# First FFN's up projection: a quad's first weights in a tile of their own, one weight sum by GpSimd, the last product on the banks of its sum

## The chip, the core and the metric

The kernel runs on one core of one Trainium2 chip. The metric is the device time of one launch in microseconds, as the median of three runs. The engines are named as the profile names them: PE is TensorE (PEld its weight loads), DVE is VectorE, ACT is ScalarE, POOL is GpSimd, and SP is SyncE, which here only issues DMAs. Each engine runs its instructions in the order in which they stand in the program. An instruction whose operand is not there yet holds up all that stand behind it on its engine.

## What is computed

One transformer layer for 256 context tokens and 256 latent tokens of width 2048: a SwiGLU feed-forward half step, a token mixer (attention and an mLSTM), and a second feed-forward half step. The change touches the first feed-forward:

```python
def half_step_ffn(x, mod, i, g, w_up, w_down):
    h = adaln(x, g, mod, i)
    a, b = jnp.split(h @ w_up, 2, axis=-1)
    return x + 0.5 * mod[:, i + 2, None, :] * ((jax.nn.silu(a) * b) @ w_down)
```

It runs on both token streams, so on 512 tokens, with `w_up` of 2048 x 11264 and `w_down` of 5632 x 2048. The vectors `mod` (nine shifts, scales and gates for each stream) are products of a condition vector with a 2048 x 18432 matrix, and they are needed only later, which is why part of their work is put beside the up projection.

## The kernel before

All matrix products are done in float32 precision by splitting each operand into a high part `hi` and a remainder `lo` (`split`, L94): ScalarE writes `hi`, VectorE writes `lo = raw - hi`, both for 128x1024 at a time, and `mm3` (L122) issues three matmuls, hi with hi, hi with lo, lo with hi. The `hi` and `lo` tiles have four buffers each, so two weight tiles of 128x2048 are split at any time.

The hidden dimension is cut into 11 blocks of 512 columns. Block 0 is done early; blocks 1 to 10 are each done by one call of `quad(n)` (L749). A quad multiplies the tokens (two halves of 128 for each stream `s`) by the gate columns (`ab` = 0) and the value columns (`ab` = 1) of its block, with the depth of 2048 in two halves. That would be eight block products; a Winograd scheme does it with seven, at the price of sums of tokens (`n1`, `s2`, `s4`, `s3`, made once) and sums of weights (made in each quad). `order` (L806) lists the seven; each runs in two steps, `q` = 0 and 1, one 1 MB weight tile a step, so that a quad has 14 steps. A step is 24 matmuls of 128x512. Steps are counted 0 to 13 below.

The weights of a quad are eight tiles, `part(n, ab, c)` (L658), c = 0..3 along the depth. Two tiles `chain_[0]` and `chain_[1]` hold the running sums. They start as part (0, q) (`first_chain`, L661), are used by product 0, get (1, q) added by an accumulating DMA that GpSimd's queue issues (`accum`, L642), are used by product 2, get (1, 2+q) added, are used by product 4, get (0, 2+q) added and are used by product 6. After that they are loaded anew for the next quad (`again`, L789). The other four tiles come into the `raw` pool of three buffers: (0, 2+q) for product 1 (`plain`, L800), (1, 2+q) for product 3 (`loaded`, L795), to which (1, q) is then added in place by an accumulating DMA for product 5. Eight accumulating DMAs and six plain ones, of 1 MB each, are thus issued in a quad.

The outputs collect in PSUM banks X, Y and Z, one for each stream. `p1` and `c11` make the gate value of the first token half, `p35` and `c12` (L770) its value part, and their product is queued in `turn`. `kept` and `c22` (L775) make the value part of the second half: `c22` adds X into `cy` on VectorE and copies X into `ca` on ScalarE. Product 6 goes to fresh banks Y, and `c21` (L780) adds Y to `ca`, takes SiLU, and multiplies. `turned` (L731) transposes a finished tile on TensorE and stores it to DRAM.

Beside it runs `side` (L835), made by `mod_items` (L195): 96 items, each a load of 128x1024 of the modulation matrix into `sraw` (two buffers, SP's queue, L212) and two multiply-and-accumulate instructions on VectorE, one for each stream's condition vector in `cBh` (`mod_half`, L180). Their product itself is not wanted; it is written as bf16 to a `c12` tile (`junk`), the same two-buffer pool from which `p35` takes `cb`. One step of `side` is taken at each step of a quad (`after`, L822); the pace is given as (items, steps), and `WAIT` more steps are left after each load of condition vectors (L178). VectorE keeps these instructions in program order. `Beside` (L249) and `mod_late` (L242) use the same `WAIT` and `mod_half` in the mixer and in the second feed-forward.

The down projection (`pair`, L945) has the same seven products for pairs of blocks. There `x3` adds X to two column blocks of the accumulator, and `c21` adds Y, product 6's fresh banks, to one of them.

Of the kernel before, what the change touches and what calls it, by code (L numbers as in the profile page):

```python
# [11 lines left out]
BF16 = mybir.dt.bfloat16  # L12
# [20 lines left out]

WAIT = 2
BLOCKS = ((0, 2), (2, 4), (4, 8), (8, 12), (12, 16))
# [13 lines left out]
def tile_layer(ctx: ExitStack, tc: tile.TileContext, I: dict, out: bass.AP):  # L49
# [130 lines left out]
    def mod_half(raw, cB, junk, i, seqs, kt, h):  # L180

        for s in seqs:
            ins = nc.vector.scalar_tensor_tensor(junk() if junk else raw, raw, 1.0, cB[s], op0=ALU.mult, op1=ALU.mult, accum_out=mT[:, i, s, kt, h : h + 1])  # L183
            tc.keep_in_program_order(ins)
# [434 lines left out]
    def pinned(ins):  # L619
        tc.keep_in_program_order(ins)  # L620
# [22 lines left out]
    with pool(name="f1u", bufs=1) as f1u:  # L643
# [5 lines left out]
        def ca_tile():  # L649
            return f1u.tile([P, CB], F32, tag="ca", name="ca", bufs=2)  # L650
# [7 lines left out]
        def part(n, ab, c):  # L658
            return I["w_up1b"][n - 1, ab, c]

        def first_chain(n, c):  # L661
            nc.sync.dma_start(chain_[c], part(n, 0, c))

# [85 lines left out]
        def quad(n, after=lambda step: None):  # L749

            X, Y, Z = {}, {}, {}
            ca, cy, cb, ra = {}, {}, {}, {}

# [21 lines left out]
            def c22(s):  # L775
                add(cy[s], X[s], cy[s])
                ca[s] = ca_tile()
                nc.scalar.activation(ca[s], X[s], AF.Copy)

            def c21(s):  # L780
                add(ca[s], Y[s], ca[s])
                nc.scalar.activation(ca[s], ca[s], AF.Silu)
                mul(ca[s], ca[s], cy[s])
                turn.append((n, 2 * s + 1, ca[s]))
# [9 lines left out]

            def loaded(q):  # L795
                ra[q] = raw_tile()
                nc.sync.dma_start(ra[q], part(n, 1, 2 + q))
                return ra[q]

            def plain(q):  # L800
                r = raw_tile()
                nc.sync.dma_start(r, part(n, 0, 2 + q))
                return r

            held = lambda q: chain_[q]
            order = (  # L806
                (a11, held, X, True, chained(1, 0), p1),
                (a12, plain, Z, True, None, c11),
                (n1, held, Y, True, chained(1, 2), kept),
                (s4, loaded, Y, False, lambda q: accum(ra[q], part(n, 1, q)), p35),  # L810
                (s2, held, X, False, chained(0, 2), c12),
                (s3, lambda q: ra[q], X, False, None, c22),
                (a22, held, Y, True, again, c21),
            )
            for m, (a, src, dst, fresh, then, use) in enumerate(order):
                if fresh:
                    dst.update({s: bank() for s in range(2)})
                for q in range(2):
                    wt = split(src(q))
                    if then:  # L820
# [13 lines left out]
        cond = Conditions(lambda h: h, lambda h: conditions(halves, h, h + 1), lambda h: halves)  # L834
        side = mod_items(half_items(2, 5), nc.sync.dma_start, sraw, 2, cond, lambda: c12_tile().bitcast(BF16), ((96, (NB - 2) * 14 + 2),))  # L835

# [19 lines left out]

        raws, place0 = [], []
        quad(1, first_steps)
        for n in range(2, NB - 1):
# [85 lines left out]
    def pair(p):  # L945
# [36 lines left out]
        def x3(c, s):  # L982
            put(2 * s + 1, 2 * c, X[c, s], True)
            put(2 * s + 1, 2 * c + 1, X[c, s])
            through_gate(2 * s + 1, 2 * c + 1)

        def c21(c, s):
            put(2 * s + 1, 2 * c, Y[c, s])
            through_gate(2 * s + 1, 2 * c)
# [10 lines left out]
        def b22(c):  # L1000
# [14 lines left out]
            ("s3", lambda c: ra[c], X, False, None, x3),  # L1015
            ("a22", held, Y, True, again, c21),
        )
# [863 lines left out]
```

## Time and profile before

| what | value |
|---|---|
| time, median of 3 runs (lowest to highest) | 2709.36 us (2709.25 to 2710.56) |
| the profiled execution's own time | 2715.45 us |
| its span, first to last instruction | 2713.7 us |
| mean granted TensorE clock | 0.990 |
| ScalarE busy, share of the span | 1270.5 us, 47% |
| VectorE busy, share of the span | 1993.7 us, 73% |
| GpSimd busy, share of the span | 177.0 us, 7% |
| HBM read | 626.31 MB |

The profile is of one execution. Its views give, for each engine, the busy time, groups of equal instructions, and the idle time before an instruction with the event that ended it ("waited for"). A window is a stretch in us from the span's start; its row gives the busy time of each engine, the granted TensorE clock and the mean share of time in which the core's 16 DMA engines were busy. Matmuls are pipelined, so a matmul's own duration is longer than the distance to the next one. A DMA row gives the time from issue to landing, which includes waiting behind other transfers.

### The profile page before, as it was taken

The numbers are of one execution on the slowest core, as the hardware profiler recorded it, in microseconds if no ns is written. First come the engines' busy times: TensorE is split into PE (matmuls) and PEld (weight loads), VectorE is DVE, ScalarE is ACT, GpSimd is POOL, SyncE is SP. The second block draws the span as 40 slices with busy tenths as digits, with TensorE's granted clock in tenths as the row PEclk, the third lists the DMA queues.
The fourth block names the chain that finished last, engine by engine and source line by source line (L and its number), as shares of the span: only waits on it lengthen the run. The fifth ranks groups of instructions, "written<-read, shape, count | busy, mean of one in ns | idle before, by whom it ended". The sixth has DMA issues, their size and how long they took to land. (4 is left out here: it accounts for less than half of the span.)

```text
span 2713.7 us, 33046 instructions
## 1 busy us (share of the span) xinstructions
PE 2635.2 (97%) x12573; PEld 2173.0 (80%) x12573; DVE 1993.7 (73%) x2740; ACT 1270.5 (47%) x1592; POOL 177.0 (7%) x223
## 2 busy tenths in 40 slices
PE   6999999999999999999999999999999999999998
PEld 3588878787888778888889888877898888888886
DVE  2387777777878788888886989787675665666557
ACT  3444444444445455444454346355564444444444
POOL 0000001100101000000110000120000000000000
PEclk8999999999999999999999999999999999999999
DMA  8879999998999989888986867574566666666553
GB/s 354 315 231 251 246 271 263 253 277 240 267 261 273 267 235 247 211 219 224 234 244 230 310 229 239 186 250 154 190 233 219 225 226 222 222 227 217 211 196 128
DMA packets 125311, 644.27 MB, mean 237 GB/s; under 512 B 13400, under 2 KB 17496, under 8 KB 67680
## 3 DMA queue, kind: packets, MB, share of 16 engines
q1 hardware_dynamic: 104704, 508.98, 51.8%
q0 software_dynamic: 20448, 133.18, 24.8%
q8 instruction: 99, 1.62, 0.2%
q14 instruction: 60, 0.49, 0.1%
HBM read 626.31 MB, written 15.79 MB: 237 GB/s over the span
## 5 line engine op out<-in xcount | busy, mean ns | idle before, releaser
L103 DVE TENSOR_TENSOR lo<-raw,hi 128x1024 fp32r<-128x1024 f32 (+3 forms) x600 | 720.0, 1206 | 400.0 <-ACT hi L102 385.5
L102 ACT ACTIVATE hi<-raw 128x1024 fp32r<-128x1024 f32 (+3 forms) x600 | 624.6, 1044 | 762.5 <-PE mm L126 628.1
L125 PE MATMUL mm<-lo,hhi 128*128 128x512 f32 (+3 forms) x1024 | 391.3, 382 | 17.0 <-DVE lo L103 16.9
L124 PE MATMUL mm<-hi,hhi 128*128 128x512 f32 (+3 forms) x1024 | 392.1, 386 | 0.0
L126 PE MATMUL mm<-hi,hlo 128*128 128x512 f32 (+3 forms) x1024 | 389.5, 380 | 0.0
L102 ACT ACTIVATE hi<-chain 128x1024 fp32r<-128x1024 f32 x240 | 252.1, 1058 | 266.7 <-PE mm L126 127.0
L103 DVE TENSOR_TENSOR lo<-chain,hi 128x1024 fp32r<-128x1024 f32 x240 | 289.9, 1222 | 104.0 <-ACT hi L102 101.9
L183 DVE SCALAR_TENSOR_TENSOR c<-sraw,cBh 128x1024 bf16<-128x1024 f32 x192 | 229.6, 1220 | 43.0 <-DMA sraw<-in_w_mt 33.2
L124 PE MATMUL mm<-hi,h2hi 128*128 128x512 f32 x640 | 249.3, 390 | 0.0
L126 PE MATMUL mm<-hi,h2lo 128*128 128x512 f32 x640 | 249.2, 389 | 0.0
L125 PE MATMUL mm<-lo,h2hi 128*128 128x512 f32 x640 | 249.2, 389 | 0.0
L125 PEld LDWEIGHTS mm<-lo,hhi 128*128 128x128 f32 x1024 | 194.1, 190 | 54.0 <-DVE lo L103 23.1
L126 PEld LDWEIGHTS mm<-hi,hlo 128*128 128x128 f32 x1024 | 193.8, 189 | 33.6 <-issue 0.2
L124 PEld LDWEIGHTS mm<-hi,hhi 128*128 128x128 f32 x1024 | 193.1, 189 | 31.4
L124 PE MATMUL mm<-hhi,hi 128*128 128x512 f32 (+1 forms) x384 | 142.0, 371 | 1.2 <-ACT hi L102 1.2
L124 PEld LDWEIGHTS mm<-hi,h2hi 128*128 128x128 f32 x640 | 120.2, 188 | 25.1
L126 PEld LDWEIGHTS mm<-hi,h2lo 128*128 128x128 f32 x640 | 120.2, 188 | 24.9
L125 PEld LDWEIGHTS mm<-lo,h2hi 128*128 128x128 f32 x640 | 120.2, 188 | 24.8
L124 PE MATMUL mm<-hi,hid2h 128*128 128x512 f32 x352 | 138.6, 396 | 0.0
L126 PE MATMUL mm<-hhi,lo 128*128 128x512 f32 (+1 forms) x384 | 137.6, 360 | 1.0 <-DVE lo L103 1.0
L125 PE MATMUL mm<-hlo,hi 128*128 128x512 f32 (+1 forms) x384 | 138.1, 360 | 0.0
L126 PE MATMUL mm<-hi,hid2l 128*128 128x512 f32 x352 | 137.2, 390 | 0.0
(383 smaller groups left out, 4745.7 us busy)
## 6 DMA issues: line engine op xcount, KB each, us to landing
raw<-in_w_up2b SPq DMA_DIRECT2D x80, 1024.0 KB, 4.7
raw<-in_w_dn SPq DMA_DIRECT2D x70, 1024.0 KB, 4.8
sraw<-in_w_mt SPq DMA_DIRECT2D x128, 512.0 KB, 6.4
chain<-in_w_up1b POOLq DMA_DIRECT2D x60, 1024.0 KB, 11.1
raw<-in_w_up1b SPq DMA_DIRECT2D x40, 1024.0 KB, 8.5
sr<-in_w_mt SPq DMA_DIRECT2D x69, 512.0 KB, 5.2
mraw<-in_w_m SPq DMA_DIRECT2D x32, 1024.0 KB, 7.5
chain<-in_w_dn POOLq DMA_DIRECT2D x30, 1024.0 KB, 8.6
```

The costliest lines, as they stand in the source:

```text
L102: nc.scalar.activation(hi, src, AF.Copy)
L103: nc.vector.tensor_tensor(lo, src, hi.bitcast(F32), op=ALU.subtract)
L124: nc.tensor.matmul(out_ap, sh, mh, start=first, stop=False, skip_group_check=skip)
L125: nc.tensor.matmul(out_ap, sh, ml, start=False, stop=False, skip_group_check=skip)
L126: nc.tensor.matmul(out_ap, sl, mh, start=False, stop=last, skip_group_check=skip)
L183: ins = nc.vector.scalar_tensor_tensor(junk() if junk else raw, raw, 1.0, cB[s], op0=ALU.mult, op1=ALU.mult, accum_out=mT[:, i, s, kt, h : ...
```

## The change

In the first feed-forward's up projection:

- The tile of a quad's first product is no longer the chain. `load` puts part (0, 0), (0, 1) and (0, 2) of the next quad into `raw` buffers at steps 8, 11 and 12, and part (0, 3), (1, 2) and (1, 3) of this quad at steps 1, 2 and 4; the table `loads` fixes where they stand. Three loads are issued ahead of the first quad.
- The chain starts as part (1, q). Part (0, q) is added by an accumulating DMA at steps 0 and 1, which no longer has to wait for a split of the chain.
- The sum with part (1, 2+q) is made by GpSimd as an addition in SBUF of 128x2048 (`twice`, steps 6 and 7), from the `raw` tile that product 3 uses, and no longer by an accumulating DMA. The accumulating DMA into that `raw` tile follows it. A quad now has six accumulating DMAs, eight plain ones and two GpSimd additions.
- Product 6 accumulates on the banks X. `c22` no longer copies X, and `c21` applies SiLU to X itself.
- The second of an item's two multiply-and-accumulate instructions writes its product over the `sraw` tile, in float32.
- `WAIT` is 3 in place of 2, and the pace of `side` is 96 items in four steps fewer.

In the down projection, product 6 accumulates on X too, and one of the additions into the accumulator goes.

```diff
@@ -31,7 +31,7 @@
 PACE = 0.5
 
 
-WAIT = 2
+WAIT = 3
 BLOCKS = ((0, 2), (2, 4), (4, 8), (8, 12), (12, 16))
 FB = 4
 CB = 512
@@ -180,7 +180,7 @@
     def mod_half(raw, cB, junk, i, seqs, kt, h):
 
         for s in seqs:
-            ins = nc.vector.scalar_tensor_tensor(junk() if junk else raw, raw, 1.0, cB[s], op0=ALU.mult, op1=ALU.mult, accum_out=mT[:, i, s, kt, h : h + 1])
+            ins = nc.vector.scalar_tensor_tensor(raw if s == seqs[-1] else junk(), raw, 1.0, cB[s], op0=ALU.mult, op1=ALU.mult, accum_out=mT[:, i, s, kt, h : h + 1])
             tc.keep_in_program_order(ins)
 
     def mod_sum(dst, i, s, kk):
@@ -659,7 +659,14 @@
             return I["w_up1b"][n - 1, ab, c]
 
         def first_chain(n, c):
-            nc.sync.dma_start(chain_[c], part(n, 0, c))
+            nc.sync.dma_start(chain_[c], part(n, 1, c))
+
+        raw_of = {}
+
+        def load(n, ab, c):
+            if n < NB:
+                raw_of[n, ab, c] = raw_tile()
+                nc.sync.dma_start(raw_of[n, ab, c], part(n, ab, c))
 
         for c in range(2):
             first_chain(1, c)
@@ -749,7 +756,7 @@
         def quad(n, after=lambda step: None):
 
             X, Y, Z = {}, {}, {}
-            ca, cy, cb, ra = {}, {}, {}, {}
+            ca, cy, cb = {}, {}, {}
 
             def p1(s):
                 ca[s] = ca_tile()
@@ -774,12 +781,10 @@
 
             def c22(s):
                 add(cy[s], X[s], cy[s])
+
+            def c21(s):
                 ca[s] = ca_tile()
-                nc.scalar.activation(ca[s], X[s], AF.Copy)
-
-            def c21(s):
-                add(ca[s], Y[s], ca[s])
-                nc.scalar.activation(ca[s], ca[s], AF.Silu)
+                nc.scalar.activation(ca[s], X[s], AF.Silu)
                 mul(ca[s], ca[s], cy[s])
                 turn.append((n, 2 * s + 1, ca[s]))
 
@@ -792,30 +797,30 @@
                 else:
                     nc.sync.dma_start(chain_[q], I["w_dn1"][0, 2 * q])
 
-            def loaded(q):
-                ra[q] = raw_tile()
-                nc.sync.dma_start(ra[q], part(n, 1, 2 + q))
-                return ra[q]
-
-            def plain(q):
-                r = raw_tile()
-                nc.sync.dma_start(r, part(n, 0, 2 + q))
-                return r
+            def twice(q):
+
+                ra = raw_of[n, 1, 2 + q]
+                pinned(nc.gpsimd.tensor_tensor(chain_[q], chain_[q], ra, op=ALU.add))
+                accum(ra, part(n, 1, q))
 
             held = lambda q: chain_[q]
+            raw = lambda ab, c: lambda q: raw_of[n, ab, c + q]
+            loads = {1: (n, 0, 3), 2: (n, 1, 2), 4: (n, 1, 3), 8: (n + 1, 0, 0), 11: (n + 1, 0, 1), 12: (n + 1, 0, 2)}
             order = (
-                (a11, held, X, True, chained(1, 0), p1),
-                (a12, plain, Z, True, None, c11),
-                (n1, held, Y, True, chained(1, 2), kept),
-                (s4, loaded, Y, False, lambda q: accum(ra[q], part(n, 1, q)), p35),
+                (a11, raw(0, 0), X, True, chained(0, 0), p1),
+                (a12, raw(0, 2), Z, True, None, c11),
+                (n1, held, Y, True, None, kept),
+                (s4, raw(1, 2), Y, False, twice, p35),
                 (s2, held, X, False, chained(0, 2), c12),
-                (s3, lambda q: ra[q], X, False, None, c22),
-                (a22, held, Y, True, again, c21),
+                (s3, raw(1, 2), X, False, None, c22),
+                (a22, held, X, False, again, c21),
             )
             for m, (a, src, dst, fresh, then, use) in enumerate(order):
                 if fresh:
                     dst.update({s: bank() for s in range(2)})
                 for q in range(2):
+                    if 2 * m + q in loads:
+                        load(*loads[2 * m + q])
                     wt = split(src(q))
                     if then:
                         then(q)
@@ -832,7 +837,7 @@
 
         halves = [cBh[:, q, :] for q in range(2)]
         cond = Conditions(lambda h: h, lambda h: conditions(halves, h, h + 1), lambda h: halves)
-        side = mod_items(half_items(2, 5), nc.sync.dma_start, sraw, 2, cond, lambda: c12_tile().bitcast(BF16), ((96, (NB - 2) * 14 + 2),))
+        side = mod_items(half_items(2, 5), nc.sync.dma_start, sraw, 2, cond, lambda: c12_tile().bitcast(BF16), ((96, (NB - 2) * 14 - 2),))
 
         def first_steps(step):
             if step in (1, 2, 3, 4, 5, 6):
@@ -855,6 +860,8 @@
                 split_to(place0[step - 11], quarters(raws[step - 11].bitcast(F32))[0])
 
         raws, place0 = [], []
+        for c in range(3):
+            load(1, 0, c)
         quad(1, first_steps)
         for n in range(2, NB - 1):
             quad(n, lambda step: steps(side))
@@ -980,12 +987,11 @@
             through_gate(2 * s, 2 * c + 1)
 
         def x3(c, s):
-            put(2 * s + 1, 2 * c, X[c, s], True)
             put(2 * s + 1, 2 * c + 1, X[c, s])
             through_gate(2 * s + 1, 2 * c + 1)
 
         def c21(c, s):
-            put(2 * s + 1, 2 * c, Y[c, s])
+            put(2 * s + 1, 2 * c, X[c, s], True)
             through_gate(2 * s + 1, 2 * c)
 
         def loaded(m, cb):
@@ -1013,7 +1019,7 @@
             ("s4", b22, Y, False, lambda c: accum(ra[c], w(0, 2 * c + 1)), p35),
             ("s2", held, X, False, lambda c: accum(chain_[c], w(1, 2 * c)), c12),
             ("s3", lambda c: ra[c], X, False, None, x3),
-            ("a22", held, Y, True, again, c21),
+            ("a22", held, X, False, again, c21),
         )
         todo = first_plan if p == 0 else plan if p < NP - 1 else last_plan
         for m, (g, src, dst, fresh, then, use) in enumerate(order):
```

## The prediction, made before the changed kernel had run

> **What bounds the kernel now.** I first read the page's busy shares, then the first feed-forward in windows: quads, each from its first matmul on `n1` to the next quad's, then all of them in one, then the down projection.
>
> ```profile
> PE 2635.2 (97%) x12573; PEld 2173.0 (80%) x12573; DVE 1993.7 (73%) x2740; ACT 1270.5 (47%) x1592; POOL 177.0 (7%) x223
> ```
>
> ```profile
> core 0: us, PE busy (x) PEld busy (x) DVE busy (x) ACT busy (x) POOL busy (x), PEclk, DMA share, GB/s
> 193.40:271.50 78.10, 78.10 (x353) 64.67 (x352) 57.30 (x69) 37.97 (x44) 7.01 (x8) 1.00 0.94 242
> 349.90:432.00 82.10, 80.05 (x353) 65.83 (x352) 64.31 (x82) 37.88 (x44) 6.95 (x8) 0.98 0.95 266
> 594.20:680.90 86.70, 80.36 (x353) 65.67 (x352) 61.93 (x78) 37.61 (x43) 7.03 (x8) 0.98 0.91 248
> 193.40:987.00 793.60, 770.70 (x3419) 632.66 (x3418) 617.59 (x786) 370.64 (x427) 67.79 (x77) 0.99 0.95 259
> 985.00:1410.00 425.00, 423.76 (x1879) 350.44 (x1877) 362.40 (x411) 212.59 (x237) 51.22 (x60) 1.00 0.90 231
> ```
>
> TensorE sets the end. A quad in which it never waits takes 78.1 us (first window): 14 steps of 5.6 us with the transposes, 5.4 without. The stretch 193.4 to 987.0 holds nine whole quads and the last ten steps of a tenth, 78.1 x (9 + 10/14) = 758.7 us by that measure. It took 793.6. So 34.9 us are lost here, and that is all the change can win in this stage. The DMA engines are busy 0.95 of it. The down projection has nothing to win: PE is busy 423.76 of 425.
>
> The waits in the up projection (160 to 990) say who is late, TensorE's first, then VectorE's: us, times, longest.
>
> ```profile
> PE mm L125 <- DVE lo L103: 22.1, 10, 5.2
> ```
>
> ```profile
> DVE lo L103 <- ACT hi L102: 122.5, 86, 4.0
> DVE c L183 <- DMA sraw<-in_w_mt: 33.2, 15, 7.8
> DVE c L183 <- DMA cBh<-ccd: 9.4, 2, 5.0
> ```
>
> TensorE waits ten times, always for a `lo`. VectorE is not short of time (617.59 of 793.6 us busy); it is held by its order. One such stall in time order, on VectorE and then on TensorE:
>
> ```profile
> 387.24 1.22 DVE L183 SCALAR_TENSOR_TENSOR c<-sraw,cBh 128x1024 bf16<-128x1024 f32 x1
> ...
> 390.52 1.23 DVE L183 SCALAR_TENSOR_TENSOR c<-sraw,cBh 128x1024 bf16<-128x1024 f32 x1 [2.05 <-DMA sraw<-in_w_mt]
> ...
> 392.82 1.22 DVE L103 TENSOR_TENSOR lo<-raw,hi 128x1024 fp32r<-128x1024 f32 x1
> ```
>
> ```profile
> 394.09 0.80 PE L125 MATMUL mm<-lo,hhi 128*128 128x512 f32 x1 [2.05 <-DVE lo L103]
> 394.69 0.63 PE L126 MATMUL mm<-hi,hlo 128*128 128x512 f32 x1
> 395.11 0.63 PE L124 MATMUL mm<-hi,hhi 128*128 128x512 f32 x1
> ```
>
> A modulation item waits 2.05 us for its `sraw`, the `lo` behind it is late, and TensorE stands 2.05 us. Afterwards matmuls start 0.42 us apart instead of 5.4/24 = 0.23: the granted clock is down for a while (PEclk 0.98 in that quad). The quad is the one of 82.1 us, 4.0 too long, so 1.9 go to the slow clock.
>
> By the Trainium skill (TensorE: Matmul & The Clock Gate, What's actually happening) the clock falls after an idle window of about 3.4 us; here it falls after 2.05, so I follow the trace. By the page, stalls as short as those priced below would cost only themselves.
>
> **The change, part by part.** *DMA.* Each quad swaps two accumulating DMAs for two plain ones of 1 MB, 2.1 million bytes. Queues and landings of the up projection (250 to 985), then the down projection's:
>
> ```profile
> q0 software_dynamic: 10333, 75.22, 51.6%
> q1 hardware_dynamic: 26586, 116.11, 43.0%
> ...
> chain<-in_w_up1b POOLq DMA_DIRECT2D x53, 1024.0 KB, 11.3
> sraw<-in_w_mt SPq DMA_DIRECT2D x90, 512.0 KB, 6.9
> raw<-in_w_up1b SPq DMA_DIRECT2D x33, 1024.0 KB, 9.0
> ```
>
> ```profile
> chain<-in_w_dn POOLq DMA_DIRECT2D x30, 1024.0 KB, 8.6
> ```
>
> Of 735 us, q0 (accumulating) takes 51.6% for 75.22 MB, 5.04 us a MB of all 16 engines; q1 takes 43.0% for 116.11 MB, 2.72. The swap frees 2.1 x 2.32 = 4.9 us a quad, 6% of 80: the share falls from 0.95 to 0.89, about the down projection's 0.90. There the same accumulating DMA lands in 8.6 us, not 11.3. Scaled alike, `sraw` lands in 6.9 x 8.6/11.3 = 5.2 us, 1.7 sooner. The 15 waits for it are 2.2 us in the mean, so 0.77 of them goes. Against this, the six `raw` loads of a quad stand in SP's queue ahead of items' loads and wait there for a buffer, as four do now. This is the part I trust least: nothing and everything are its ends.
>
> *WAIT = 3* delays the first item after a load of condition vectors by one step.
>
> ```profile
> 606.59 1.23 DVE L183 SCALAR_TENSOR_TENSOR c<-sraw,cBh 128x1024 bf16<-128x1024 f32 x1 [4.37 <-DMA cBh<-ccd]
> ```
>
> ```profile
> 612.85 1.23 DVE L183 SCALAR_TENSOR_TENSOR c<-sraw,cBh 128x1024 bf16<-128x1024 f32 x1 [5.02 <-DMA cBh<-ccd]
> ```
>
> ```profile
> 615.27 0.50 PE L125 MATMUL mm<-lo,s4h 128*128 128x512 f32 x1 [4.37 <-DVE lo L103]
> ```
>
> Both waits are shorter than a step, so the stall of 4.37 us at 615.27 goes, and 1.9 of slow clock with it: **-6.3**. Of the other 34.9 - 6.3 = 28.6 us, 0.77 goes: **-22.0**. In the mixer and the second feed-forward the same shift moves items among idle VectorE time; I take 0, between -3 and +3.
>
> *GpSimd's additions*, twenty of 128x2048. No such row exists. The nearest are one of 128x512 and a tiny instruction for the start-up; then VectorE's `lo` under the first; then a GpSimd instruction beside a run of VectorE's:
>
> ```profile
> 1793.39 1.29 POOL L1482 TENSOR_TENSOR gm<-gm,mg 128x512 f32<-128x512 f32 x1 [14.44 <-ACT gm L1481]
> 1730.13 0.19 POOL L131 TENSOR_SCALAR rstd<-hss 128x2 f32<-128x2 f32 x1 [19.08 <-DVE hss L1435]
> ```
>
> ```profile
> 1793.51 2.25 DVE L103 TENSOR_TENSOR lo<-raw,hi 128x1024 fp32r<-128x1024 f32 x1
> ```
>
> ```profile
> 1863.83 3.44 POOL L131 TENSOR_SCALAR rstd<-hss 128x4 f32<-128x4 f32 x1 [6.75 <-DVE hss L1435]
> ```
>
> ```profile
> 1864.26 1.23 DVE L103 TENSOR_TENSOR lo<-raw,hi 128x1024 fp32r<-128x1024 f32 x1
> 1865.39 0.69 DVE L1453 TENSOR_TENSOR sq<-sq,xn 128x512 f32<-128x512 f32 x1
> 1865.99 1.23 DVE L103 TENSOR_TENSOR lo<-raw,hi 128x1024 fp32r<-128x1024 f32 x1
> ```
>
> Four times 1.29 is 5.2 us; with the start-up counted once, 4.6. I take 4.9. What they do to VectorE matters more: the `lo` that starts under the addition takes 2.25 us, not 1.23; it moves only when GpSimd is done (1794.68). And a GpSimd instruction of some 0.2 us takes 3.44 while VectorE runs without a gap. So the two exclude each other when both operands lie in SBUF, and each addition stops the splits and the modulation items for 4.9 us.
>
> The Trainium skill (GPSIMD Engine Reference, Performance versus the Vector engine) has 4.497 us for an addition of 2048 float32; by it the lateness in the walk below turns into 0.3 us in hand, and the sum is some 2 us lower.
>
> On average there is room: a quad has 64 us of VectorE work (second window), so 14 of 78.1 are free, against 2 x 4.9. Whether it fits in place shows only a walk. I take the first addition through the quad of the second window, in the built program's order. The old rows there:
>
> ```profile
> 345.75 1.23 DVE L103 TENSOR_TENSOR lo<-chain,hi 128x1024 fp32r<-128x1024 f32 x1 [0.16 <-ACT hi L102]
> 346.89 1.22 DVE L183 SCALAR_TENSOR_TENSOR c<-sraw,cBh 128x1024 bf16<-128x1024 f32 x1
> ...
> 348.03 0.69 DVE L743 TENSOR_TENSOR ca<-mm,ca 128x512 f32<-128x512 f32 x1
> ```
>
> The chain's split ends at 346.98, which frees the addition; an item's first half holds VectorE to 348.03; then comes `ca<-mm,ca`, one operand in PSUM, and GpSimd gets in, until 352.9. The item's second half ends at 354.1 (1.14 us each, 346.89 to 348.03), the first `lo` of step 5 at 355.2 and, after one more `ca` (0.6), the second at 357.0. Step 4 began at 349.9, so step 5 wants them at 349.9 + 5.4 + 0.2 = 355.5 and, six matmuls on, at 356.9. That is 0.1 us late; 0.2 in hand with 4.6, 0.4 late with 5.2. The second addition, behind the accumulating DMA of step 6, ends in the same way just before step 8. I take 0.3 us for each, for items that come late themselves: **+6**. The ends are 0 and 1.5 (one more item half, 1.14, ahead of the `lo`), so 0 to 30.
>
> *Behind it on POOL.* The accumulating DMA for step 11 is issued after the second addition, 5 us later than now. Its landing (8.6 to 11.3 us) meets a cover of about 10: 0 to 1.5 us a quad, I take 0.3: **+3**.
>
> *Banks.* Product 6 now waits until `c22` has read X. In VectorE's order that addition stands behind the first `lo` of step 12 by one item half and itself, 1.14 + 0.6: 0 to 1.7 us a quad. I take 0.3: **+3**. The next quad's X waits for SiLU on ScalarE, with half a step (2.7 us) in hand.
>
> *At nothing:* the copies that ScalarE loses and the additions that VectorE loses at the end of a quad (0.69 each), since no stall above stands behind them; the first weights' `raw` loads, issued three steps (16 us) or more ahead of their use and landing in 9.0 (a late one would cost its lateness, once a quad); the item's product written into `sraw`, which is read first and reloaded as before; the down projection's lost addition, since TensorE does not wait there.
>
> Sum: -6.3 - 22.0 + 6 + 3 + 3 = -16.3, from the profiled execution's 2715.45 to 2699.1. That execution lies 6.1 above the median of the runs, so **2693**.
>
> **Rivals.** *Everything hides:* all 34.9 us go and the new waits cost nothing: 2709.4 - 34.9 = 2674.5. For it: the walk ends within 0.4 us of the need. Against: items still share VectorE's order.
>
> *The relief does not reach:* two `sraw` buffers and SP's order set the waits, not the DMA share. Then only 6.3 is won and the new waits cost 6 to 12: 2709 to 2715. For it: SP holds items' loads behind `raw` loads today as well.
>
> *Slower, by the exclusion:* GpSimd enters later, or lasts longer, so that each addition stops TensorE by 2 us, 40 in all and not 6: 2693 + 34 = 2727. It decides from 1.1 us an addition on, (16.3 + 6)/20. For it: the 2.25 and the 3.44 above. Against: it needs 1.6 us beyond the walk.
>
> **The numbers.** Forecast 0.45 (its own range 2680 to 2703), everything hidden 0.15, no relief 0.17, slower 0.23. About 0.2% (5.4 us) is what a measurement of this kernel tells from no change. Faster: 0.45 + 0.15 = 0.60. Same: 0.14 out of the third. Slower: 0.03 of it and 0.23, so 0.26. The range goes from 2676 to 2720; outside lie the tip of the best case and half of the slower one.
>
> **What would show it.** DMA share 0.89 in the quads, `sraw` landing near 5.2 us and the chain's accumulating DMA near 9; VectorE's waits for `sraw` a quarter of 33.2, none for `cBh` over 1 us; GpSimd rows of 4.6 to 5.2 us with a `lo` or item half under each that takes that much longer; quads of 79 to 81 us. Quads above 82 with TensorE waiting at steps 5, 6 or 8 mean the exclusion; a wait at step 12 for `cy` means the banks; `sraw` waits of 2 us as before mean no relief. Each of these makes the prediction wrong.

## The result, and the profile after

| | before | after |
|---|---|---|
| median of the runs, same chip | 2709.96 us (2709.25 to 2712.36, 4 runs) | 2774.44 us (2771.97 to 2779.0, 4 runs) |
| ratio, 95% interval | | 1.0238 [1.0221, 1.0256] |
| profiled execution, span | 2713.7 us | 2777.3 us |
| up projection, first matmul on `n1` to first on `hidh` | 793.6 us | 846.7 us |
| from there to the end of the span | 1726.7 us | 1734.5 us |

The change makes the kernel 2.4% slower: 64 us, where I had forecast 16 won. Of the 63.6 us by which the spans differ, 53.1 lie in the up projection, 2.7 ahead of it and 7.8 behind it.

The page's busy shares, then the windows of after: three quads and the whole stretch, with the columns of the windows shown before.

```profile
PE 2659.9 (96%) x12573; PEld 2181.0 (79%) x12573; DVE 2044.4 (74%) x2700; ACT 1256.4 (45%) x1568; POOL 261.3 (9%) x223
```

```profile
196.10:276.00 79.90, 78.44 (x353) 64.56 (x353) 58.52 (x61) 36.98 (x42) 14.47 (x9) 1.00 0.81 230
276.00:362.00 86.00, 80.78 (x353) 65.50 (x353) 70.01 (x79) 36.90 (x42) 12.83 (x8) 0.98 0.81 235
884.80:977.00 92.20, 84.00 (x353) 67.32 (x352) 74.27 (x89) 38.83 (x44) 16.88 (x9) 0.94 0.84 246
196.10:1042.80 846.70, 788.10 (x3424) 636.78 (x3423) 683.61 (x772) 361.44 (x409) 147.09 (x79) 0.98 0.82 241
```

Only the first quad, in which the modulation items begin at step 8, comes near the forecast. The other whole quads take 85 to 92 us. VectorE is busy 66 us longer than before (683.61 against 617.59) with 14 instructions fewer, and the DMA share has fallen to 0.82, further than I had said. The relief came, and the time did not follow it. Waits of the stage (160 to 1045), TensorE's and VectorE's:

```profile
DVE lo L103 <- ACT hi L102: 97.0, 70, 6.1
DVE c L183 <- DMA sraw<-in_w_mt: 54.9, 17, 8.2
PE mm L125 <- DVE lo L103: 40.4, 24, 4.1
ACT hi L102 <- DMA raw<-in_w_up1b: 22.0, 5, 6.3
PE mm L124 <- DVE cy L750: 12.5, 5, 3.3
```

TensorE's waits for `lo` have gone from 22.1 us to 40.4, there is a new one for `cy` (the banks), and VectorE's waits for `sraw` went up, not down to a quarter. The wait for `cBh` is gone, as forecast. ScalarE's 22.0 us of waits for a raw load are new: before, it waited for up-projection weights only where they go into the chain (43.6 us, now 5.3). Landings (250 to 1040):

```profile
q1 hardware_dynamic: 29660, 136.88, 46.7%
q0 software_dynamic: 7732, 56.27, 36.0%
...
raw<-in_w_up1b SPq DMA_DIRECT2D x50, 1024.0 KB, 12.0
sraw<-in_w_mt SPq DMA_DIRECT2D x92, 512.0 KB, 6.4
chain<-in_w_up1b POOLq DMA_DIRECT2D x35, 1024.0 KB, 12.2
```

`sraw` lands in 6.4 us (6.9 before, 5.2 forecast), the raw loads in 12.0 (9.0), the chain's accumulating DMA in 12.2 (11.3, 9 forecast). The groups of GpSimd's additions and of the items' second products in after:

```profile
L803 POOL TENSOR_TENSOR chain<-chain,raw 128x2048 f32<-128x2048 f32 x20 | 100.3, 5016 | 229.5 <-DVE lo L103 229.5
```

```profile
L183 DVE SCALAR_TENSOR_TENSOR sraw<-sraw,cBh 128x1024 f32<-128x1024 f32 x96 | 165.5, 1724 | 1.5
```

An addition takes 5.0 us, as forecast. A second product takes 1.72 us in the mean and not 1.22; some of them lie under an addition. One such place in time order, the first addition of the quad that starts at 362.0:

```profile
362.35 1.22 DVE L183 SCALAR_TENSOR_TENSOR c<-sraw,cBh 128x1024 bf16<-128x1024 f32 x1
362.52 5.53 POOL L803 TENSOR_TENSOR chain<-chain,raw 128x2048 f32<-128x2048 f32 x1 [20.66 <-DVE lo L103]
...
363.50 0.69 DVE L750 TENSOR_TENSOR ca<-mm,ca 128x512 f32<-128x512 f32 x1
364.10 5.03 DVE L183 SCALAR_TENSOR_TENSOR sraw<-sraw,cBh 128x1024 f32<-128x1024 f32 x1
...
369.06 1.21 DVE L103 TENSOR_TENSOR lo<-chain,hi 128x1024 fp32r<-128x1024 f32 x1
...
370.33 0.50 PE L125 MATMUL mm<-lo,n1h 128*128 128x512 f32 x1 [2.47 <-DVE lo L103]
```

This is the walk of the prediction, in the order of its instructions: GpSimd gets in while `ca` is added, whose one operand lies in PSUM; the item's second half then holds VectorE for 5.03 us and not 1.22; the `lo` behind it is late and TensorE stands 2.47 us. The walk had the order right. It had VectorE 3.4 us earlier against TensorE: there the addition began 1.9 us ahead of step 4, here it gets in at 363.5, 1.5 behind the step's start at 362.0. What made VectorE late lies a little ahead of it in the same trace, at the split for step 3:

```profile
354.30 2.01 ACT L102 ACTIVATE hi<-raw 128x1024 fp32r<-128x1024 f32 x2 [6.29 <-DMA raw<-in_w_up1b]
...
355.39 2.36 DVE L103 TENSOR_TENSOR lo<-raw,hi 128x1024 fp32r<-128x1024 f32 x2 [5.91 <-ACT hi L102]
```

The load of part (0, 3) takes over the `raw` buffer of the first weights. It was issued at 338.55, with step 0, and landed at 354.19, 15.6 us later; ScalarE stood 6.29 us for it and VectorE 5.91 behind that. In seven of the nine whole quads of after, the first addition starts 0.4 to 1.5 us behind the start of step 4.

For every late start of a matmul (0.9 us or more behind the one before it, in place of 0.23) I added up the excess by step, from the quads' matmuls in the traces; places where transposes stand are not counted. Steps with at most 2.5 us are left out.

| kernel | step 3 | 5 | 7 | 10 | 11 | 12 | up projection, us |
|---|---|---|---|---|---|---|---|
| before | 0 | 0 | 7.4 | 0 | 13.3 | 2.1 | 793.6 |
| after | 5.9 | 13.4 | 14.7 | 0 | 6.5 | 18.7 | 846.7 |
| before, GpSimd's additions alone | 0 | 2.7 | 19.4 | 0 | 13.8 | 9.6 | 827.4 |
| before, loads alone | 3.2 | 0 | 5.1 | 0 | 20.4 | 10.5 | 819.8 |
| after, sum left out | 3.8 | 0 | 0 | 0 | 8.6 | 8.6 | 792.7 |
| after, items not held at step 8 | 0 | 6.6 | 16.8 | 15.6 | 0 | 2.2 | 817.5 |

### The profile page after: what moved, and what is told of

Same layout as the page of the kernel before. It is cut to its first block, busy times and chain, and to the rows that moved or that the text cites. A ratio compares the mean times of both kernels' runs of the same rounds, so it can differ in the third digit from the quotient of the medians.

```text
span 2777.3 us, 32887 instructions
## 1 busy us (share of the span) xinstructions
PE 2659.9 (96%) x12573; PEld 2181.0 (79%) x12573; DVE 2044.4 (74%) x2700; ACT 1256.4 (45%) x1568; POOL 261.3 (9%) x223
## 5 line engine op out<-in xcount | busy, mean ns | idle before, releaser
L103 DVE TENSOR_TENSOR lo<-raw,hi 128x1024 fp32r<-128x1024 f32 (+2 forms) x640 | 782.6, 1230 | 435.8 <-ACT hi L102 421.1
L102 ACT ACTIVATE hi<-raw 128x1024 fp32r<-128x1024 f32 (+2 forms) x640 | 665.6, 1044 | 809.1 <-PE mm L126 632.8
L102 ACT ACTIVATE hi<-chain 128x1024 fp32r<-128x1024 f32 x200 | 210.2, 1059 | 202.9 <-PE mm L126 114.8
L103 DVE TENSOR_TENSOR lo<-chain,hi 128x1024 fp32r<-128x1024 f32 x200 | 251.9, 1274 | 64.0 <-ACT hi L102 63.2
L183 DVE SCALAR_TENSOR_TENSOR sraw<-sraw,cBh 128x1024 f32<-128x1024 f32 x96 | 165.5, 1724 | 1.5
L183 DVE SCALAR_TENSOR_TENSOR c<-sraw,cBh 128x1024 bf16<-128x1024 f32 x96 | 117.0, 1219 | 55.3 <-DMA sraw<-in_w_mt 54.9
L124 PEld LDWEIGHTS mm<-hi,h2hi 128*128 128x128 f32 x640 | 120.1, 188 | 25.2
```

The costliest lines, as they stand in the source:

```text
L102: nc.scalar.activation(hi, src, AF.Copy)
L103: nc.vector.tensor_tensor(lo, src, hi.bitcast(F32), op=ALU.subtract)
L124: nc.tensor.matmul(out_ap, sh, mh, start=first, stop=False, skip_group_check=skip)
L183: ins = nc.vector.scalar_tensor_tensor(raw if s == seqs[-1] else junk(), raw, 1.0, cB[s], op0=ALU.mult, op1=ALU.mult, accum_out=mT[:, i, s ...
```

## The experiments

Each ratio is against runs of the kernel before on the same chip, with its 95% interval. "Stage" is the up projection as in the table above, from each run's own profile, against 793.6 us. Each stage is of one execution, and 25 executions of the kernel before on one chip lay between 2705.5 and 2726.0 us, so a stage that differs by a few us is not told from an equal one. The ratios are the firmer numbers.

**Parts of the change, each alone in the kernel before**

*GpSimd's additions* (`b_gpsum`):

```diff
-                (n1, held, Y, True, chained(1, 2), kept),
-                (s4, loaded, Y, False, lambda q: accum(ra[q], part(n, 1, q)), p35),
+                (n1, held, Y, True, None, kept),
+                (s4, loaded, Y, False, twice, p35),   # add ra[q] to chain_[q] on GpSimd, then accum
```

> The kernel before with one thing alone: the accumulating DMAs chained at steps 4 and 5 become GpSimd additions of the s4 weights at steps 6 and 7, ahead of the accumulating DMA into those weights. Theory 1: 2745 to 2775, with VectorE instructions of 5 us beside the additions. Theories 2 and 3: 2700 to 2720, since banks and the order of SP's queue are those of before and the DMA engines have less to do.

2746.8 us, ratio 1.0111 [1.0090, 1.0132], stage +33.8 us: theory 1, at its low end. The items' products in this run, and the same group before:

```profile
L183 DVE SCALAR_TENSOR_TENSOR c<-sraw,cBh 128x1024 bf16<-128x1024 f32 x192 | 305.0, 1613 | 24.6 <-DMA sraw<-in_w_mt 24.3
```

```profile
L183 DVE SCALAR_TENSOR_TENSOR c<-sraw,cBh 128x1024 bf16<-128x1024 f32 x192 | 229.6, 1220 | 43.0 <-DMA sraw<-in_w_mt 33.2 <-DMA cBh<-ccd 9.4
```

The same 192 products hold VectorE 75.4 us longer. The waits for `sraw` did fall (33.2 to 24.3): this much of the relief is there, and it weighs little. The table says which addition costs here: two of the stalls lie at step 5, behind the first addition (2.7 us), eight at step 7, behind the second (19.4). Without the new loads, the first addition starts 2.8 us ahead of step 4 in six of the nine whole quads, and none of the six has a stall at step 5. The second one in time order:

```profile
365.57 2.35 DVE L103 TENSOR_TENSOR lo<-raw,hi 128x1024 fp32r<-128x1024 f32 x2
...
367.84 1.21 DVE L183 SCALAR_TENSOR_TENSOR c<-sraw,cBh 128x1024 bf16<-128x1024 f32 x1
368.56 0.89 POOL L642 DMA_DIRECT2D raw<-in_w_up1b  x1 [9.17 <-issue]
...
368.99 6.18 DVE L183 SCALAR_TENSOR_TENSOR c<-sraw,cBh 128x1024 bf16<-128x1024 f32 x1
369.19 4.89 POOL L806 TENSOR_TENSOR chain<-chain,raw 128x2048 f32<-128x2048 f32 x1
...
375.10 2.35 DVE L103 TENSOR_TENSOR lo<-raw,hi 128x1024 fp32r<-128x1024 f32 x2
...
376.37 0.64 PE L125 MATMUL mm<-lo,s4h 128*128 128x512 f32 x1 [2.97 <-DVE lo L103]
```

On POOL the accumulating DMA into the s4 weights stands between the two additions. It may not write them before step 6 has split them (the `lo` that end at 367.9), and is issued 9.17 us after the end of the first addition. The second starts only at 369.19. Step 7 wants its first `lo` at 373.2, 4.0 us later, less than an addition takes. At the first addition of this quad (353.86) there were 8.4 us to step 5 at 362.3.

*The loads* (`b_loads`): the table of loads, raw tiles for the first weights, the chain started with `part(1, q)`; sums, banks, WAIT and pace as before.

> The kernel before with the loads alone: a quad's first weights in raw tiles of their own, the six raw loads at the places of the changed kernel, the chain started with the other weights; sums, banks, WAIT and pace as before. The accumulating DMA for the sum left 26 us over the kernel before in the changed kernel, and this run asks whose they are. Theory L (items' loads stand behind more raw loads in SP's queue): VectorE's waits for `sraw` 45 us or more, raw landings 11 to 12 us, ratio 1.003 to 1.008. Theory B (the banks): ratio 0.998 to 1.002, waits for `sraw` near 33 us. Neither expects an instruction of VectorE over 1.3 us.

Ratio 1.0120 [1.0092, 1.0149], stage +26.2: theory L by its waits and landings, and more time than it gave. Queues and landings (250 to 985):

```profile
q0 software_dynamic: 10174, 74.17, 49.4%
q1 hardware_dynamic: 28248, 130.46, 47.6%
...
raw<-in_w_up1b SPq DMA_DIRECT2D x50, 1024.0 KB, 11.9
sraw<-in_w_mt SPq DMA_DIRECT2D x89, 512.0 KB, 9.3
```

Two loads of 1 MB more a quad, and the queues take 97% of the DMA engines' time; `sraw` lands in 9.3 us and VectorE's waits for it are 73.4 us. Is it their bytes, or their places ahead of the items' loads? `b_loads_late` issues the same loads at the steps of the kernel before:

```diff
-            loads = {1: (n, 0, 3), 2: (n, 1, 2), 4: (n, 1, 3), 8: (n + 1, 0, 0), 11: (n + 1, 0, 1), 12: (n + 1, 0, 2)}
+            loads = {2: (n, 0, 2), 3: (n, 0, 3), 6: (n, 1, 2), 7: (n, 1, 3), 12: (n + 1, 0, 0), 13: (n + 1, 0, 1)}
```

> The kernel with the loads alone (1.012), its six raw loads issued at the steps where the kernel before has its own (2, 3, 6, 7, and 12, 13 for the next quad): the same bytes, other places in SP's queue. Theory Q (the places: two raw loads ahead of the items' loads at steps 1, 2 and 11, 12): ratio 1.002 to 1.006. Theory S (2.1 MB more a quad fill DMA engines that were busy 0.95 of the time): the share stays 0.96 or more, ratio 1.009 to 1.015.

Ratio 1.0116 [1.0095, 1.0138], DMA share 0.96, `sraw` 9.5 us: theory S. The places are not the cause. Whether it is the bytes on the DMA engines or the three `raw` buffers, which six tiles of a quad share here in place of four, no run separates.

*Product 6 on the banks of its sum* (`b_xbanks`): `c22` without its copy, `c21` with SiLU of X, `(a22, held, X, False, ...)`.

> The kernel before with product 6 of a quad alone moved onto the banks of its sum (up projection only). Theory B: waits of TensorE for `cy` of 10 us or more in the stage and slow clock after them, ratio 1.003 to 1.008. Theory L: waits for `cy` come only where VectorE is late for another reason, so 0 to 6 us of them, ratio 0.999 to 1.003.

Ratio 0.9979 [0.9963, 0.9994], or 5.7 us less; the ratio lies just below theory L's range. In the two profiled executions the stage differs by 12.6 us (781.0). Waits (160 to 980):

```profile
DVE c L183 <- DMA sraw<-in_w_mt: 26.9, 12, 5.9
PE mm L125 <- DVE lo L103: 13.5, 9, 5.9
...
PE mm L124 <- DVE cy L743: 0.3, 2, 0.2
```

Alone, this part costs no bank wait (0.3 us), as theory L has it. The two late starts at step 7 (7.4 us) are gone as well. That the spared copies and additions do that is likely, but no run separates it from the shift of the items' order that comes with them.

*WAIT 3 and the pace* (`b_wait`), *the product in place* (`b_inplace`), each by its one line of the diff:

> The kernel before with WAIT 3 and the pace of the changed kernel alone. By my prediction the stall of 4.37 us behind the condition vectors goes with its slow clock, ratio 0.9975 to 0.9985, no waits for cBh over 1 us. A rival, that items 3.6% denser give more waits for `sraw`: 1.001 to 1.004 with waits of 40 us or more.

> The kernel before with the second product of an item written over its weights in place of the spare tile, alone. By my prediction nothing: 0.9985 to 1.0015. A rival, that the weights' tile comes free later or items are no longer held back by the spare tiles: 1.002 to 1.006 with more waits for `sraw`.

`b_wait`: 1.0005 [0.9990, 1.0020], stage 788.0, 5.6 less, with no waits for `cBh`: near the 6.3 us of the prediction, in one execution each. But waits for `sraw` rise to 46.7 us, the rest of the program takes 1.6 us more, and the runs show no gain. `b_x_wait`, product 6 on X with WAIT 3 and the old pace, says the same of the whole program:

> The kernel before with product 6 on the banks of its sum, and WAIT 3 with the old pace. If the stall behind the condition vectors (4 to 5 us in this stage) is won without loss: ratio 0.994 to 0.9975. If the shift of the items costs as much again, as in b_wait: 0.998 to 1.001.

1.0003 [0.9988, 1.0018], stage 779.9, and 0.9979 without WAIT 3. `b_inplace`: 1.0032 [1.0014, 1.0050], stage +6.9, waits for `sraw` 44.7 us: not nothing, as I had it. Why was not tried.

The five parts add up to 33.8 + 26.2 - 12.6 - 5.6 + 6.9 = 48.7 us in the stage, against 53.1 for the change, but this does not show that each costs the same within the change. With the loads alone a quad has 16 DMAs of 1 MB; before and after have 14, since the change takes two accumulating ones away. `a_nosum` below has all parts but the additions: they would add up to 808.5 us, and it takes 792.7.

**Parts of the change taken back out of it**

*The sum*, left out (`a_nosum`), by an accumulating DMA (`a_dmasum`), by VectorE (`a_vecsum`), each in the one line:

```diff
-                pinned(nc.gpsimd.tensor_tensor(chain_[q], chain_[q], ra, op=ALU.add))
+                accum(chain_[q], part(n, 1, 2 + q))                                     # a_dmasum
+                pinned(nc.vector.tensor_tensor(chain_[q], chain_[q], ra, op=ALU.add))   # a_vecsum
```

> Leaves out GpSimd's addition of the weights (the sum that s2 and s3 need is incomplete); all else is the changed kernel. Theory 1 (the additions hold VectorE, late splits stop TensorE, its clock falls): the 100 us of GpSimd rows and most of TensorE's 40.4 us of waits for `lo` go; time 2690 to 2715, quads 79 to 81 us. Theory 2 (product 6 on the banks of its sum): the waits at step 12 stay as they are, time about 2750 to 2770. Theory 3 (raw loads stand in SP's queue ahead of the items' loads): waits of VectorE for `sraw` stay near 55 us, time 2745 to 2770.

> The sum is made by an accumulating DMA into the chain, as before the change, at the place of GpSimd's addition. Theory 1: 2695 to 2720, with the DMA share back near 0.95 and no VectorE instruction of 5 us. Theory 2: 2755 to 2770, with waits for `cy` at step 12 of 12 us as in the changed kernel. Theory 3: 2755 to 2775, since the order of SP's loads is the same and the DMA engines are busier.

> The changed kernel with its sum on VectorE in place of GpSimd, at the same place, with the same accumulating DMA behind it. Theory 1 (what costs is that GpSimd and VectorE shut each other out for 5 us): a little above the kernel without the sum (1.0018), so 1.002 to 1.007, and no instruction of VectorE between 3 and 6 us. Rival (what costs is the place, the accumulating DMA into the s4 weights coming late): 1.015 to 1.024 as with GpSimd.

| | ratio | stage, us |
|---|---|---|
| after (GpSimd) | 1.0238 [1.0221, 1.0256] | 846.7 |
| `a_vecsum` | 1.0138 [1.0112, 1.0163] | 822.3 |
| `a_dmasum` | 1.0095 [1.0073, 1.0116] | 815.9 |
| `a_nosum` | 1.0018 [1.0007, 1.0030] | 792.7 |

`a_nosum` leaves the sum out of the weights of `s2` and of product 6, which use the chain after it. Its stage is that of before (the 2721.4 us are a little above theory 1's number), so GpSimd's twenty additions cost 54 us here, 2.7 each. The late raw loads are in it too (33.5 us of ScalarE's waits for them), and cost 3.8 us at step 3. Neither theory gave the numbers of the other two. Summed by DMA, 22 us of the loss in the stage stay, near what the loads cost alone: both have 16 DMAs in a quad. Summed by VectorE, where no engine shuts the other out (its additions take 2.28 us), half the loss stays, more than theory 1's 0.7% and less than the rival's 1.5%. The waits of `a_vecsum`, and a place at step 12 that makes them:

```profile
DVE c L183 <- DMA sraw<-in_w_mt: 58.8, 17, 7.0
PE mm L124 <- DVE cy L750: 23.0, 6, 4.4
PE mm L125 <- DVE lo L103: 11.2, 10, 3.3
```

```profile
394.95 1.21 DVE L103 TENSOR_TENSOR lo<-raw,hi 128x1024 fp32r<-128x1024 f32 x1
...
399.63 1.22 DVE L183 SCALAR_TENSOR_TENSOR c<-sraw,cBh 128x1024 bf16<-128x1024 f32 x1 [3.47 <-DMA sraw<-in_w_mt]
...
400.78 1.22 DVE L103 TENSOR_TENSOR lo<-chain,hi 128x1024 fp32r<-128x1024 f32 x1
401.92 1.22 DVE L183 SCALAR_TENSOR_TENSOR sraw<-sraw,cBh 128x1024 f32<-128x1024 f32 x1
...
403.06 0.68 DVE L750 TENSOR_TENSOR cy<-mm,cy 128x512 f32<-128x512 f32 x1
...
403.89 0.77 PE L124 MATMUL mm<-hi,hhi 128*128 128x512 f32 x1 [3.23 <-DVE cy L750]
```

TensorE's wait is put down to `cy`, the banks. But VectorE stood 3.47 us for an item's weights first, and everything behind it is late by that.

*The banks* (`a_banks` in after; `a_vecsum_banks` with VectorE's sum), product 6 back on banks of its own in the up projection:

> Only the last product of a quad goes back to banks of its own, with the copy of X and the addition of before; GpSimd's additions stay. Theory 1: the 12.5 us of waits for `cy` go and with them some slow clock, but what is late behind an addition is late all the same: 2745 to 2768, quads 84 to 88 us. Theory 2: 2700 to 2725, quads 79 to 82 us.

> The changed kernel with its sum on VectorE (1.0138) and its last product back on banks of its own. Theory B2 (without the lock the bank wait of 23.0 us at step 12 is what stops TensorE): those waits go, ratio 1.001 to 1.007. Rival (the split at step 12 is late anyway, behind an item that waits for its weights, and the wait only changes its name): 1.010 to 1.015 with waits for `lo` at step 12 instead.

1.0212 [1.0193, 1.0231] (2774.2 us, above theory 1's 2768 and far from theory 2) and 1.0139 [1.0120, 1.0158], the rival's. In the second the wait for `cy` is gone and the time is the same:

```profile
DVE c L183 <- DMA sraw<-in_w_mt: 54.2, 22, 7.4
PE mm L125 <- DVE lo L103: 32.9, 26, 3.4
```

23.0 + 11.2 us under two names have become 32.9 under one. Beside VectorE's sum the bank wait was a label, not a cause.

**What the items do.** A half is one of an item's two products. I counted them over nine quads, each cut into 14 equal stretches of time, one a step. Before, no half starts on VectorE in step 8, one in step 7, 21 in step 10, 12.7 a step in the mean. Items throw one or two products away into the tiles of `c12`, which hold the sums of step 7 until step 9, so they stand still and then catch up two or three at a time, as I read it faster than two `sraw` buffers fill. This is the burst of the expectations. In after it is 0 in step 8 and 24 in step 10. A tile of their own (8-bit, never read) takes that hold away:

```diff
-... cond, lambda: c12_tile().bitcast(BF16), ...
+... cond, lambda: junkm, ...
```

> The changed kernel with a tile of its own (8-bit, never read) for the first thrown-away product of an item, all else as changed. Theory burst: the 25 us of waits at steps 11 and 12 shrink to 10 or less, those at steps 5 and 7 stay, ratio 1.012 to 1.018. Theory lock (GpSimd's additions make those as well): 1.020 to 1.026.

> The kernel before with product 6 on the banks of its sum (0.9979 alone) and a tile of its own (8-bit, never read) for the thrown-away products of the items, which took a spare tile of c12 till now and so stood still at step 8. Theory burst (items stand still at step 8, then come 23 halves in step 10 instead of 14, and VectorE meets weights that have not landed, just ahead of the splits of steps 11 and 12): waits of TensorE at steps 11 and 12 below 6 us instead of 13, up stage 762 to 775 us, ratio 0.988 to 0.995. Rival (the landing alone sets it, wherever the items stand): ratio 0.996 to 1.001, the waits moved to other steps.

In after (`a_junk`): 1.0135 [1.0115, 1.0155], 1.0% better than after, with at most 17 halves in a step. The waits at steps 11 and 12 go from 25.2 us to 2.2, and 15.6 us are new at step 10, while step 7, GpSimd's, stands at 16.8 (14.7) and step 5 at 6.6 (13.4): theory burst by its time, though a part of the waits only moved. In the kernel before with product 6 on X (`b_x_junk`): stage 778.6, 2.4 less than without the tile, and the ratio is 0.9978 [0.9968, 0.9988], the same. That is the rival's number: the waits moved to step 10, with 11.2 us in the last quad alone.

With VectorE's sum in place of GpSimd's (the lock of the expectations), in after (`a_vecsum_junk`), and in the kernel before with product 6 on X, without and with the tile (`b_vecsum_x`, `b_vecsum_x_junk`):

> The changed kernel with its sum on VectorE and a tile of its own for the first thrown-away product of an item. Theory burst (the 24 us of waits at step 12 that the sum on VectorE left came from items in a burst): ratio 1.001 to 1.006, waits at steps 11 and 12 below 8 us. Rival (the order and bytes of the loads keep the items late at all steps): 1.009 to 1.014.

> The kernel before with both sums on VectorE at step 6 and 7 and product 6 on the banks of its sum; loads, WAIT and pace as before. The DMA engines are spared two accumulating DMAs a quad and no engine is locked out; VectorE has two instructions of about 2.4 us more a quad. Theory 1 (the lock and the extra loads made the change slow, not the sum itself): `sraw` lands in about 6 us, up stage 765 to 785 us against 793.6, ratio 0.988 to 0.998. Rival (VectorE's order has no place for 2.4 us either): stalls at steps 6 and 7, ratio 1.000 to 1.008.

> The kernel before with the sums on VectorE, product 6 on the banks of its sum and a tile of its own for the items' thrown-away products; loads, WAIT and pace as before. Theory burst (the spared accumulating DMAs had no effect since the items came in a burst): up stage 765 to 776 us, ratio 0.991 to 0.997. Rival (items wait for single loads, whatever the share): as without the sum on VectorE, 0.997 to 1.003.

`a_vecsum_junk`: 1.0036 [1.0021, 1.0050], stage 792.4: theory burst's number. Lock and burst taken away, the change costs next to nothing in this stage. `b_vecsum_x`: 1.0029 [1.0018, 1.0040], stage 791.3: the rival's number, but with its stalls at steps 11 and 12 and not at 6 and 7. `b_vecsum_x_junk`: 1.0008 [0.9995, 1.0020], the rival's. Its stretch, below that of `b_x_junk`, which has the accumulating DMAs:

```profile
195.60:974.20 778.60, 763.24 (x3423) 629.52 (x3422) 615.54 (x773) 365.52 (x409) 68.74 (x78) 0.99 0.96 264
```

```profile
194.70:987.10 792.40, 767.69 (x3423) 631.07 (x3422) 654.52 (x793) 365.50 (x409) 52.07 (x59) 0.99 0.82 233
```

The DMA share falls from 0.96 to 0.82 and the stage grows by 13.8 us: the spared DMAs are not worth the 39 us of VectorE.

*One addition in place of two* (`b_gpsum_q0`: `b_gpsum` with GpSimd adding for q = 0 alone, an accumulating DMA at step 7 for q = 1):

> The kernel before with GpSimd adding only for the first of the two chains (step 6); the second is summed by an accumulating DMA as before, issued at step 7. With both additions, eight of nine whole quads stopped TensorE at step 7 (19.4 us of waits) and two at step 5 (2.7 us). Theory P (the second addition is the costly one, since on POOL it stands behind an accumulating DMA that waits for the split of step 6): waits at step 7 at or below those of the kernel before (7.4 us), ratio 0.997 to 1.004. Theory U (each addition costs alike, 1.7 us): ratio 1.005 to 1.007.

Ratio 1.0103 [1.0087, 1.0118]: neither number. The waits at steps 5 and 7 are gone altogether, as theory P has it, but those at 11 and 12 grew to 26.2 and 11.8 us: the accumulating DMA that I moved from step 5 to 7 lands, as I read it, among the items of the burst (`sraw` 7.5 us, longest wait 9.5). The run settles which addition stops TensorE and not what one addition is worth.

A version faster than both kernels: the kernel before with product 6 on the banks of its sum, 0.9979 [0.9963, 0.9994], or 0.9978 [0.9968, 0.9988] with the tile for the items' products.

## Why the prediction was wrong

Two steps of the sum failed. The larger is *"GpSimd's additions, +6"*, taken up below: in the changed kernel they cost 54 us (846.7 against 792.7 without them), which is all that the change loses in this stage (by the ratios, 1.0238 against 1.0018 without them). The other is why nothing was won against them.

*That step is "0.77 of 28.6 us, -22.0"*: that a lower DMA share brings `sraw` sooner and that waits shrink with it. No run shows it to be worth anything in the stage: `a_nosum`, whose DMAs are those of the change, has a share of 0.87 and the time of before; `b_vecsum_x_junk`, with 39 us more work on VectorE, has 0.82 and more time than at 0.96. I had scaled a median of landings by another stage's. From the issue and landing of each `sraw` load (250 to 960): before, 23 loads issued with no accumulating DMA in flight land in 5.3 us in the mean, 40 with one in 7.7, 15 with two in 11.0. In `a_nosum` it is 39, 32 and 13 loads at 4.7, 9.3 and 14.3 us. More loads meet no accumulating DMA and the median falls (6.9 to 6.3), but those that do land later, and where one is in flight there are 1.2 plain loads of 1 MB beside it in the mean, not 0.6. The mean goes from 7.7 to 7.9. My second rival, "the relief does not reach", was right about this.

*"The first weights' raw loads at nothing"*: I asked whether the first weights land in time, and not what they do to the loads behind them. Part (0, 3) gets its buffer at step 0 and takes up to 16 us to land, not 9.0 (the place at 354.30); TensorE waits 5.9 us at step 3, and VectorE is late for step 4. Alone, beside the two accumulating DMAs that the change takes away, the loads cost 26.2 us in the stage. Without the additions the stage shows no loss by them (`a_nosum`).

*"GpSimd's additions, +6"*: the length was right (4.6 to 5.7 us), and so was the walk of the first as long as VectorE runs where it ran before: 2.7 us of waits in `b_gpsum`. In the changed kernel it starts behind step 4 and step 5 loses 13.4 us. The late raw loads stand in front of it in the trace; that they are the reason is argued from there, since no run has the additions and all else of the change without these loads. The sentence "the second addition ... ends in the same way just before step 8" failed. It stands on POOL behind a DMA that waits for step 6's split, and meets the split of step 7. I had named that DMA as late *behind* the addition and not asked what it holds back ahead of it. Alone the additions cost 33.8 us, 1.7 each, near the 2 us of the rival "slower, by the exclusion"; in the changed kernel, where VectorE runs later, 2.7. That rival had the sign and the mechanism and kept my -22.

By the Trainium skill (SBUF — State Buffer, Who interferes with whom) a VectorE instruction with two inputs in SBUF and a GpSimd instruction that reads SBUF contend for a shared port that is held by an exclusive lock, and a VectorE instruction with at most one SBUF input, outside of its two-port modes, does not contend. The trace agrees on both: 1.22 became 5.03 us, while `ca`, with an operand in PSUM, kept its 0.69.

*"Banks, +3"*: alone they win, 0.21% by the ratio (5.7 us). Taken out of after, the time is 0.26% lower (1.0212 against 1.0238, with intervals that overlap), and beside VectorE's sum it is the same. The wait for `cy` at step 12, which I had named as the sign of the banks, came and did not mean them there. The +3 for the accumulating DMA behind the second addition has no run of its own.

*"-6.3" for WAIT*: near it in the stage (-5.6), without a gain that the runs can tell. *"At nothing" for the product in place*: 0.32% by the ratio, 6.9 us in the stage.

*"And 1.9 of slow clock with it"*, as a share of each stall: of the 53.1 us, 38.1 are late starts (60.9 against 22.8, the sums over all steps), and the other 15 lie in the matmuls between them. Most of that is slow clock: the traces show it granted at half for 41.0 us of the stage after and 17.1 before, which is 12 us lost. It does not follow each stall: before, five of eight have it at or behind them, each for 3.4 us.

Left open: the 7.8 us behind the stage, for which the forecast had nothing. They lie in the down projection, from its first matmul on `hidh` to its last: 429.8 us before, 437.7 after. All kernels with WAIT 3 or with the tile for the items' products take 432.6 to 438.4 us there, all others 429.3 to 430.9. The order is clear, its cause is open. Open too is the 2.7 us ahead of it: the starts of the stage vary from 193.4 to 196.4 us over all kernels.

## What to carry to other kernels

An average share of the DMA engines is no price: look up, load by load, what is in flight when the load that someone waits for is issued. An instruction on a shared queue costs twice: for what waits behind it, and for what the instruction ahead of it makes it wait for; with an exclusive resource, compare its length with the time to the next instruction that must not be late. And where the same stall returns at the same steps under changing names, look for who stands still before it.

## What the runs showed of the hardware

- GpSimd needs 5.02 us for an addition of 128x2048 beside VectorE's work (4.6 to 5.7); VectorE needs 2.28 for the same one.
- Of each addition VectorE lost 3.8 us in its products alone (75.4 us for 20 additions).
- A load of 512 KB takes 5.3 us in the mean with no accumulating DMA in flight and 2.4 to 3.3 us more for each one (before).
